# An even layer's gated unit, moved from ahead of its dilated attention to the attention's last heads

## The chip, the cores and the metric

The kernel runs on one core of one Trainium2 chip. The metric is the device time of one execution in microseconds; the kernel before has a median of 4341.29 us over three runs (4339.98 to 4341.60).

## The reference, cut to what matters

The program is two blocks one after the other. The change concerns the even layer of the second block, on 1024 tokens of width 1024:

```python
def mixer_even(h, pos, w_in, gmlp_norm, w_s, b_s, w_out):
    q, k, v, z = split(h @ w_in, [768, 1536, 2304])          # 12 heads of 64, z: 512 columns
    q, k = partial_rope(q), partial_rope(k)
    a_out = dilated_mixture(q, k, v)                          # 768 columns
    g_out = spatial_gating(z, gmlp_norm, w_s, b_s)            # 256 columns
    return concatenate([a_out, g_out]) @ w_out

def spatial_gating(z, v_norm, w_s, b_s):
    u, vv = split(gelu(z), 2)                                 # 256 columns each, 4 groups of 64
    vv = rmsnorm(vv, v_norm)                                  # over the 64 of each group
    mixed = einsum('gpq,bnqgc->bnpgc', w_s, vv) + b_s         # over the 128 tokens of a chunk
    return u * mixed
```

`dilated_mixture` joins three banded softmax attentions (dilations 1, 4 and 16) by their log-sum-exps.

## The kernel before, in words

The program states its operations in one order, and a tile scheduler that simulates time gives every engine its own queue from that; each engine then runs its queue in order. Tiles come from pools. A pool opened late stands where an earlier one was, so its first tile waits until the earlier one is closed.

All projections are products of fp32 numbers split in two: `split_into` (L98, L99) casts a tile to a high part on ACT and takes the rest on DVE or POOL, and `mm3` (L91 to L93) sums three partial matmuls. `proj_N` takes one projection of 128 tokens to 256 columns: 8 parts of the depth times 3, that is 24 matmuls; this is a *step* here. Weights come by `whalf` (L114) into `wraw` and are cast to `whi` and `wlo`.

Attention (`even_attn`) runs 12 heads of 8 *units*: four units of near keys (`near`, L1311) and four of keys of the same class mod 4 (`same_class`, L1319); four units are a half head here. A unit scores two tiles into a bank `ps` (four matmuls), takes the row maxima with the table of bands `tab` on DVE (L1361), the exps on ACT (L1364), turns the weights on PE (`pt`, L1328), splits them (L98, L99) and multiplies by the values (`po`, L1377 and L1389). Behind each unit, `step(unit)` runs what the table `order` holds for it. `plan(unit, n, *steps)` (L1282) fills the table: of the query and key pairs (`P[1]` to `P[5]`, two heads each) eight projection steps and four stacks at 16i-20 and 16i-8, of the value groups `V[1]` and `V[2]` (four heads each) eight steps at units 4 and 36, one step a unit. Pair 0 and V[0] stand in `order[-1]`, ahead of the first unit:

```python
        plan(4, 1, *V[1])
        plan(36, 1, *V[2])
        def step(unit):
            for f in order.get(unit, ()):
                f()
        step(-1)
        s2 = between()
        tab = s2.tile([128, 1152], F32, name="tab")
```

The gated unit (`even_gmlp`, L1123 to L1174) is stated before all of that. Its projections run up to the `yield` through `next(gmlp)` (16 steps, 384 matmuls, with gelu at the copy out of PSUM, L1129), partly in the tail of the MLP of the block ahead; the rest (norm of `vv`, mixing `pm`, the product with `u`, L1165, four transposes a time into `pzt` and the copy to `zo`, L1172) runs in `between()`, after pair 0 and V[0] and before the pool `eb` opens, from which `tab`, the values and the softmax tiles come. Its rows go to `eD`, the DRAM buffer from which the output projection reads. `by_class` sorts tokens by their class mod 4.

PSUM has one bank for the pairs' projections and stacks (`pj`), three banks under the tag "s" (`mb`: scores `ps`, projections of V, before also of z and the mixing), and the banks of `pt` and `po`. A pair of V steps (u = 0 and 1) shares one bank `mb`, taken by the first and freed by the copy behind the second. At the end, `last()` closes the pool of activations (`he`) and fetches and casts the rows of w_out.

Of the kernel before, what the change touches and what calls it, by code (L numbers as in the profile page):

```python
# [6 lines left out]
F32 = mybir.dt.float32  # L7
# [11 lines left out]
NT = 8  # L19
# [7 lines left out]
class Kern:  # L27
# [1095 lines left out]
    def even_gmlp(self, hT, w, dst, sp, W2):  # L1123

        nc, a = self.nc, self.a
        zz = []
        for i in range(2):
            z = sp.tile([128, NT, 256], F32, name="z%d" % i)
            self.proj_N2(self.w256(w, 2304 + 256 * i, W2 if i else None), hT, lambda t2, p: nc.scalar.activation(  # L1129
                z[:, 2 * t2:2 * t2 + 2, :], p, AF.Gelu_apprx_tanh), self.mb)  # L1130
            zz.append(z)
        yield
        self.exp_ln_table()
        u, vv = zz
        grow = self.row(a["even_gmlp_norm_2"], 256, "zg", sp)
        sq = sp.tile([128, NT, 256], F32, name="zsq")
        ss = sp.tile([128, 32], F32, name="zss")
        rs = sp.tile([128, 32], F32, name="zrs")
        nc.gpsimd.tensor_tensor(sq, vv, vv, op=ALU.mult)
        v32 = lambda x: x.rearrange("p t (g c) -> p (t g) c", g=4)  # L1140
        nc.vector.tensor_reduce(out=ss, in_=v32(sq), axis=AX.X, op=ALU.add)
        self.rstd(ss, 64, rs)
        nc.vector.tensor_tensor(v32(vv), v32(vv), rs[:, :, None].to_broadcast([128, 32, 64]), op=ALU.mult)
        nc.gpsimd.tensor_tensor(vv, vv, grow[:, None, :].to_broadcast([128, NT, 256]), op=ALU.mult)
        ws = sp.tile([128, 4, 128], F32, name="zws")
        for c in range(4):
            nc.sync.dma_start(ws[32 * c:32 * c + 32], dap(a["even_w_spatial_2"], 128 * c,
                                                          [[512, 32], [128 * 128, 4], [1, 128]]))
        br = sp.tile([4, 128], F32, name="zbr")
        nc.sync.dma_start(br, a["even_b_spatial_2"][0])  # L1150
        ws, br = self.by_class(ws, sp, "zwc"), self.by_class(br[:, None, :], sp, "zbq")[:, 0, :]
        p = self.tp("pws")
        for g in range(4):
            nc.tensor.transpose(p[:, g, :], ws[:, g, :], self.ident)
        wt = sp.tile([128, 4, 128], F32, name="zwt")
        nc.vector.tensor_copy(wt, p)
        p = self.tp("pbs")
        nc.tensor.transpose(p[:, 0, 0:4], br, self.ident[0:4, 0:4])
        bc = sp.tile([128, 4], F32, name="zbc")
        nc.vector.tensor_copy(bc, p[:, 0, 0:4])  # L1160
        for g in range(4):
            p = self.mb("pm").rearrange("p (t c) -> p t c", t=NT)
            gs = slice(g * 64, (g + 1) * 64)
            nc.tensor.matmul(p, wt[:, g, :], vv[:, :, gs], start=True, stop=True)
            nc.vector.scalar_tensor_tensor(sq[:, :, gs], p, bc[:, g:g + 1], u[:, :, gs], op0=ALU.add, op1=ALU.mult)  # L1165
        for i in range(2):
            o = sp.tile([128, 1024], F32, name="zo", tag="zo", bufs=1)
            for g in range(2):
                p = self.tp("pzt")
                for t in range(4):  # L1170
                    nc.tensor.transpose(p[:, t, :], sq[:, 4 * g + t, i * 128:(i + 1) * 128], self.ident)
# [10 lines left out]
    def even_attn(self, hT, w, dst, s1, W2, between, last):  # L1182
# [99 lines left out]
        def plan(unit, n, *steps):  # L1282
            for i, f in enumerate(steps):
                order.setdefault(max(unit + n * i, 0), []).append(f)
# [904 lines left out]
```

## Time and profile before

| | |
|---|---|
| median of 3 runs | 4341.29 us (4339.98 to 4341.60) |
| the profiled execution, its own time | 4346.24 us |
| its span in the profile | 4344.5 us |
| busy: PE, DVE, ACT, POOL | 3861.5 (89%), 2440.4 (56%), 1915.9 (44%), 1149.2 us (26%) |
| granted TensorE clock, 40 slices | 0.7 to 0.9 of full speed |
| the even layer's heads | first row maximum at 2209.70 us, last at 2596.71 us |

How to read it: the span begins at 0, and every time in microseconds is counted from there. A busy PE is no proof of full speed: matmuls are pipelined. The chain that ended last is 27% PE by itself, and the even layer is about an eighth of the span, so shares over the whole span say little of it; it is read by windows.

### The profile page before, as it was taken

Reading aid. Unit: us, or ns where it says so; the run is one execution under the profiler, and the core shown is the slowest. Engines: PE = TensorE matmul, PEld = TensorE weight load, DVE = VectorE, ACT = ScalarE, POOL = GpSimd, SP = SyncE. Lnnn points to the kernel's source line nnn. Section 1 sums busy time; section 2 is a strip of 40 time slices with the busy share of each in tenths; the row PEclk is TensorE's granted clock in tenths of the full one; section 3 lists DMA queues with packets and bytes.
Section 4 is the critical chain, followed back from the end, with each engine's and each line's share of the span. In section 5 each row is a group of like instructions: output and inputs, shape, how many; then the busy total and the mean of one; then the engine's idle time right before and its main releaser. Section 6 shows DMA issues by size and latency. Waiting matters only on the chain. (4 is left out here: it accounts for less than half of the span.)

```text
span 4344.5 us, 57369 instructions
## 1 busy us (share of the span) xinstructions
PE 3861.5 (89%) x21765; PEld 3209.0 (74%) x21765; DVE 2440.4 (56%) x4070; ACT 1915.9 (44%) x3190; POOL 1149.2 (26%) x878
## 2 busy tenths in 40 slices
PE   6999978898799999998999988699895898996997
PEld 5887866666587888886899977576694787884765
DVE  6545584663344233336446673787538566736876
ACT  3444434241424211112455662366523667832765
POOL 2000041330343112124412221011024556620111
PEclk8999989989899999999899998799997999997999
DMA  4212253121543111112242333799410001036997
GB/s 167 72 51 56 85 177 102 49 99 54 203 146 97 54 44 54 44 49 80 61 120 74 85 88 128 280 377 361 150 45 9 18 8 58 19 103 248 375 356 245
DMA packets 321975, 531.40 MB, mean 122 GB/s; under 512 B 39894, under 2 KB 217441, under 8 KB 321700
## 3 DMA queue, kind: packets, MB, share of 16 engines
q1 hardware_dynamic: 312052, 492.62, 33.5%
q0 software_dynamic: 9648, 35.13, 3.2%
q8 instruction: 171, 2.80, 0.3%
q14 instruction: 104, 0.85, 0.1%
HBM read 427.39 MB, written 91.88 MB: 120 GB/s over the span
## 5 line engine op out<-in xcount | busy, mean ns | idle before, releaser
L98 ACT ACTIVATE whi<-wraw 128x1024 fp32r<-128x1024 f32 (+1 forms) x515 | 530.1, 1038 | 777.7 <-PE py L93 213.7
L99 DVE TENSOR_TENSOR wlo<-wraw,whi 128x1024 fp32r<-128x1024 f32 (+3 forms) x418 | 519.0, 1258 | 409.6 <-ACT whi L98 397.2
L99 POOL TENSOR_TENSOR wlo<-wraw,whi 128x1024 fp32r<-128x1024 f32 (+3 forms) x97 | 226.6, 2336 | 1198.0 <-ACT whi L98 1135.7
L91 PE MATMUL pj<-h,whi 128*128 128x512 f32 (+1 forms) x592 | 255.6, 432 | 44.0 <-ACT gst L791 41.8
L92 PE MATMUL mm<-h,whi 128*128 128x512 f32 x640 | 253.9, 397 | 3.0 <-POOL h L99 1.8
L91 PE MATMUL mm<-h,whi 128*128 128x512 f32 x640 | 252.7, 397 | 1.8 <-ACT ms L905 1.4
L93 PE MATMUL mm<-h,wlo 128*128 128x512 f32 x640 | 252.9, 396 | 0.8 <-POOL wlo L99 0.8
L92 PE MATMUL pj<-h,whi 128*128 128x512 f32 (+1 forms) x592 | 248.1, 419 | 0.0
L93 PE MATMUL pj<-h,wlo 128*128 128x512 f32 (+1 forms) x592 | 246.5, 416 | 0.2 <-POOL wlo L99 0.2
L91 PE MATMUL pgu<-whi,xe 128*128 128x512 f32 x512 | 207.6, 406 | 6.2 <-ACT xe L98 6.2
L927 DVE TENSOR_TENSOR Y<-py,Y 128x1024 f32<-128x1024 f32 x112 | 137.1, 1224 | 133.3 <-PE py L93 133.3
L91 PE MATMUL py<-whi,mr 128*128 128x512 f32 x512 | 201.6, 394 | 9.3 <-DVE mr L936 8.2
L93 PE MATMUL pgu<-whi,xe 128*128 128x512 f32 x512 | 205.7, 402 | 0.0
L92 PE MATMUL pgu<-wlo,xe 128*128 128x512 f32 x512 | 205.5, 401 | 0.0
L93 PE MATMUL py<-whi,mr 128*128 128x512 f32 x512 | 203.1, 397 | 0.0
L92 PE MATMUL py<-wlo,mr 128*128 128x512 f32 x512 | 202.4, 395 | 0.0
L396 PE MATMUL ptp<-ident,e 128*128 128x128 f32 x1280 | 183.8, 278 | 15.1 <-ACT pf L400 6.9
L1038 DVE TENSOR_REDUCE ast<-ps 128x1 f32<-128x1024 f32 x128 | 156.4, 1222 | 69.7 <-PE ps L93 48.6
L91 PEld LDWEIGHTS pj<-h,whi 128*128 128x128 f32 (+1 forms) x592 | 118.4, 200 | 85.4 <-ACT gst L791 50.7
L396 PEld LDWEIGHTS ptp<-ident,e 128*128 128x128 f32 x1280 | 149.9, 143 | 30.8 <-ACT pf L400 13.6
L402 POOL TENSOR_TENSOR pt<-pf,pt 128x512 fp32r<-128x512 f32 x128 | 164.0, 1281 | 10.4
L99 DVE TENSOR_TENSOR pt<-ptp,pt 128x512 fp32r<-128x512 f32 x192 | 130.5, 689 | 40.2 <-ACT pt L98 38.9
(643 smaller groups left out, 11038.2 us busy)
## 6 DMA issues: line engine op xcount, KB each, us to landing
wraw<-in_moe_w_gate_dram SPq DMA_DIRECT2D x128, 512.0 KB
wraw<-in_moe_w_up_dram SPq DMA_DIRECT2D x128, 512.0 KB
wraw<-in_moe_w_down_dram SPq DMA_DIRECT2D x128, 512.0 KB
wraw<-in_mlp_w_dram SPq DMA_DIRECT2D x64, 512.0 KB
wraw<-in_w_in_dram SPq DMA_DIRECT2D x52, 512.0 KB
wad<-in_ada_w_dram SPq DMA_DIRECT2D x48, 512.0 KB
gD<-gst SPq DMA_DIRECT2D x24, 512.0 KB
wraw<-x SPq DMA_DIRECT2D x20, 512.0 KB
```

The source lines that it names most:

```text
L91: t.matmul(out, l[0], r[0], start=start, stop=False)
L92: t.matmul(out, l[0], r[1], start=False, stop=False)
L93: return t.matmul(out, l[1], r[0], start=False, stop=stop)
L98: nc.scalar.activation(hi, src, AF.Copy)
L99: (nc.gpsimd if leng == "pool" else nc.vector).tensor_tensor(lo, src, hi.bitcast(F32), op=ALU.subtract)
L396: nc.tensor.transpose(p[:, k, :], e[:, (4 * kg + k) * 128:(4 * kg + k + 1) * 128], self.ident)
L402: nc.gpsimd.tensor_tensor(lo, f, hi.bitcast(F32), op=ALU.subtract)
L927: nc.vector.tensor_tensor(y, pv, y, op=ALU.add)
L1038: nc.vector.tensor_reduce(out=st[:, 0:1], in_=pv, axis=AX.X, op=ALU.min)
```

## The change

The gated unit is no longer computed ahead of attention. `even_gmlp` and `by_class` go. Its two projections become `z_steps(1)` (the `vv` half) and `z_steps(0)` (the `u` half), eight steps each in the table, from unit 67 on, each pair of steps in a bank `mb`, copied without gelu to a tile `zs` and written to a DRAM buffer `zD`. `gated()` returns nine steps: `load` (unit 87) reads `zD` back, sorted by class through its addressing, together with the spatial weights, and applies gelu; `norm` (two halves, units 89, 90), `mix` (four groups, units 90 to 93) and `turn` (two, units 93, 94) compute the rest in the bank `pj`, in tiles that the query and key stacks no longer use. The spatial weights and biases are laid out by class and transposed beforehand, when inputs are prepared.

The table changes too: the pairs' eight projection steps are 1.5 units apart instead of 1, V[1] starts at unit 6 and V[2] at 34, both 3 units apart. The pool `eg` goes, and so does the gated unit's place in `between()`.

```diff
-    def even_gmlp(self, hT, w, dst, sp, W2):
...
-    def by_class(self, x, sp, name):
...
-        rests = [[s1.tile([128, 1024], FR, name="kl%d%d" % (i, j)) for j in range(2)] for i in range(2)]
+        rests = [[s1.tile([128, 1024], FR, name="kl%d%d" % (i, j), tag="kl%d%d" % (i, j)) for j in range(2)] for i in range(2)]
...
+        zD = self.dram.tile([1024, 512], F32, name="zD")
+        def z_steps(q):
+            wl, ps = [], []
+            def part(j):
+                i, u = divmod(j, 2)
+                if j == 0:
+                    wl.extend(self.w256(w, 2304 + 256 * q))
+                if u == 0:
+                    ps.append(self.mb())
+                self.proj_N(wl, hT, 2 * i + u, ps[0][:, u * 256:(u + 1) * 256])
+                if u == 0:
+                    return
+                z = s1.tile([128, 1024], FR, name="zs", tag="vs").bitcast(F32)[:, 0:512]
+                nc.scalar.activation(z, ps.pop(), AF.Copy)
+                nc.sync.dma_start(dap(zD, 256 * i * 512 + 256 * q, [[512, 128], [128 * 512, 2], [1, 256]]),
+                                  z.rearrange("p (u m) -> p u m", u=2))
+            return [lambda i=i: part(i) for i in range(8)]
+        def gated():
+            r = []
+            st = s1.tile([128, 2, 2, 16], F32, name="zst")
+            def load():
+                f, o = [s1.tile([128, 1024], F32, name="zf%d" % j, tag="kl0%d" % j) for j in range(2)]
+                wt, grow, bc = f[:, 0:512].rearrange("p (g t) -> p g t", g=4), f[:, 512:768], f[:, 768:772]
...
+                V = [s1.tile([128, 4, 2, 128], F32, name="zv", tag="eqk", bufs=2).rearrange("p t a b -> p t (a b)")
+                     for _ in range(2)]
+                U = [s1.tile([128, 1024], FR, name="zu", tag=n, bufs=3).bitcast(F32).rearrange("p (t m) -> p t m", t=4)
+                     for n in ("Q", "K")]
+                r.extend((U, V, o, wt, grow, bc))
+                for q, x in ((1, V), (0, U)):
+                    for g in range(2):
+                        nc.sync.dma_start(x[g], dap(zD, 512 * g * 512 + 256 * q, [[512, 128], [128 * 512, 4], [1, 256]]))
+                for x in V + U:
+                    nc.scalar.activation(x, x, AF.Gelu_apprx_tanh)
+                self.exp_ln_table()
+            def norm(g):
...
+                nc.gpsimd.tensor_tensor(sq, v, v, op=ALU.mult)
+                nc.vector.tensor_reduce(out=ss, in_=h4(sq), axis=AX.X, op=ALU.add)
+                self.rstd(ss, 64, rs)
+                nc.vector.tensor_tensor(h4(v), h4(v), rs[:, :, None].to_broadcast([128, 16, 64]), op=ALU.mult)
+                nc.gpsimd.tensor_tensor(v, v, grow[:, None, :].to_broadcast([128, 4, 256]), op=ALU.mult)
+            def mix(k):
+                U, V, o, wt, grow, bc = r
+                p = self.pj().rearrange("p (t c) -> p t c", t=NT)
+                gs = slice(k * 64, (k + 1) * 64)
+                for g in range(2):
+                    nc.tensor.matmul(p[:, 4 * g:4 * g + 4], wt[:, k, :], V[g][:, :, gs], start=True, stop=True)
+                for g in range(2):
+                    nc.vector.scalar_tensor_tensor(U[g][:, :, gs], p[:, 4 * g:4 * g + 4], bc[:, k:k + 1], U[g][:, :, gs],
+                                                   op0=ALU.add, op1=ALU.mult)
+            def turn(i):
+                o = r[2]
+                for g in range(2):
+                    p = self.pj().rearrange("p (t j) -> p t j", t=4)
+                    for t in range(4):
+                        nc.tensor.transpose(p[:, t, :], r[0][g][:, t, i * 128:(i + 1) * 128], self.ident)
+                    nc.scalar.activation(o[:, g * 512:(g + 1) * 512].rearrange("p (t j c) -> p t c j", t=4, c=4),
+                                         p.rearrange("p t (c j) -> p t c j", c=4), AF.Copy)
+                nc.sync.dma_start(dst[768 + i * 128:768 + (i + 1) * 128, :], o)
+            steps = lambda f, n: [lambda i=i: f(i) for i in range(n)]
+            return [load] + steps(norm, 2) + steps(mix, 4) + steps(turn, 2)
...
-                order.setdefault(max(unit + n * i, 0), []).append(f)
+                order.setdefault(max(unit + int(n * i), 0), []).append(f)
...
-            plan(16 * i - 20, 1, *p[0:8])
+            plan(16 * i - 20, 1.5, *p[0:8])
             plan(16 * i - 8, 1, p[8], p[10], p[9], p[11])
-        plan(4, 1, *V[1])
-        plan(36, 1, *V[2])
+        plan(6, 3, *V[1])
+        plan(34, 3, *V[2])
+        plan(67, 1.25, *z_steps(1), *z_steps(0))
+        z = gated()
+        plan(87, 1, *z[0:1])
+        plan(89, 1, *z[1:3])
+        plan(90, 1, *z[3:7])
+        plan(93, 1, *z[7:9])
...
-        sg = opn("eg")
-        gmlp = self.even_gmlp(h, a["even_w_in_2"], eD, sg, W2)
-        next(gmlp)
         T = []
         def between():
-            for _ in gmlp:
-                pass
-            cls("eg", "ew")
+            cls("ew")
             return opn("eb")
```

How the queues stand. First SP's, at the start of the layer, behind the last writes of the MLP (`x_82`). Before (`ecs` are the rotary tables, `zg`, `zws`, `zbr` the gated unit's inputs, `vD` the writes of values, `eD<-zo` the gated rows):

```order
L1004 DMA x_82<-Y 128x1024 x8
L114 DMA wraw<-in_even_w_in_dram 128x4x256 x2
L1192 DMA ecs_14238<-in_rope_even_dram 32x8x8 x4
L1192 DMA ecs_14243<-in_rope_even_dram 32x8x8 x4
L146 DMA zg<-in_even_gmlp_norm_dram 128x256
L1147 DMA zws<-in_even_w_spatial_dram 32x4x128 x2
L114 DMA wraw<-in_even_w_in_dram 128x4x256 x2
```

```order
L1272 DMA vD_14256<-vs 32x2x512 x5
L1174 DMA eD<-zo 128x1024
L371 DMA K_14516<-K_14516 64x4x128
L371 DMA K_14517<-K_14517 64x4x128
L1174 DMA eD<-zo 128x1024
L1298 DMA tab<-in_even_bands_dram 128x1152
```

And now:

```order
L1004 DMA x_82<-Y 128x1024 x8
L1133 DMA ecs_13809<-in_rope_even_dram 32x8x8 x4
L1133 DMA ecs_13814<-in_rope_even_dram 32x8x8 x4
L114 DMA wraw<-in_even_w_in_dram 128x4x256 x2
L1213 DMA vD_13827<-vs 32x2x512 x4
L114 DMA wraw<-in_even_w_in_dram 128x4x256 x2
L1213 DMA vD_13827<-vs 32x2x512
L371 DMA K_14089<-K_14089 64x4x128
L1213 DMA vD_13827<-vs 32x2x512
L371 DMA K_14090<-K_14090 64x4x128
L1213 DMA vD_13827<-vs 32x2x512 x6
L1323 DMA tab<-in_even_bands_dram 128x1152
```

The fetch of `tab` moved ahead of the last writes of values, and the first weights of V (`wraw`, 128x4x256) behind the eight loads of `ecs`.

Second ACT's queue. Before, in the layer's start, the gelus (`z<-mb`) stand in one stretch, with table loads around it and around the norm:

```order
L98 ACTIVATE he_13338<-ms 128x256 x15
L1129 ACT_TABLE_LOAD
L1129 ACTIVATE z_13812<-mb 128x512 x3
L98 ACTIVATE whi<-wraw 128x1024 x3
L1129 ACTIVATE z_13812<-mb 128x512
L98 ACTIVATE whi<-wraw 128x1024
L1129 ACTIVATE z_14025<-mb 128x512 x3
```

Now, in head 10 (`e` are exps of the softmax, `P` their split parts, `zs` a copied pair of z steps):

```order
L98 ACTIVATE P_18611<-pt 128x512
L1389 ACTIVATE e,sA<-e,sA 128x256
L98 ACTIVATE P_18695<-pt 128x512
L1258 ACT_TABLE_LOAD
L1258 ACTIVATE zv<-zv 128x1024
L1233 ACTIVATE zs<-mb 128x512
L1389 ACT_TABLE_LOAD
L1389 ACTIVATE e,sA<-e,sA 128x256 x2
L1364 ACTIVATE oAB<-po 64x512
```

A gelu (`zv`) stands between exps, with a table load ahead of it and one behind; heads 9 to 11 hold 12 such loads.

Third PE's queue in head 10, between the same-class and the near units. Before:

```order
L1319 MATMUL ps<-K_18376,Qc 128x256
L1319 MATMUL ps<-kl_14248,Qc 128x256
L1311 MATMUL ps<-K_18377,Q_18341 128x256
L1311 MATMUL ps<-kl_14249,Q_18341 128x256
L1389 MATMUL po<-P_19001,vc 128x256
L1328 MATMUL pt<-ident,e 128x128 x3
```

Now, of near units (L1336 scores, L1353 transposes):

```order
L1336 MATMUL ps<-K_18837,Q_18776 128x256
L1336 MATMUL ps<-kl_13821,Q_18776 128x256
L1353 MATMUL pt<-ident,e 128x128 x2
L92 MATMUL mb<-wlo,he_13338 128x256
L93 MATMUL mb<-whi,he_13339 128x256
L91 MATMUL mb<-whi,he_13338 128x256
L92 MATMUL mb<-wlo,he_13338 128x256
L93 MATMUL mb<-whi,he_13339 128x256
L1353 MATMUL pt<-ident,e 128x128 x2
L1336 MATMUL ps<-K_18837,Q_18776 128x256
L1336 MATMUL ps<-kl_13821,Q_18776 128x256
```

Matmuls of a z step (`mb`) now stand between a unit's transposes and the next scores.

## Rows read from the trace of the kernel before

**Rows 1.** Windows: stretch, its us, busy per engine (instructions), PE clock, DMA share, GB/s.

```profile
2100.00:2120.00 20.00, 15.22 (x108) 14.82 (x107) 5.75 (x11) 10.84 (x19) 14.21 (x16) 0.83 0.32 80
2120.00:2140.00 20.00, 20.00 (x172) 20.00 (x171) 1.93 (x3) 2.69 (x4) 1.49 (x1) 1.00 0.39 102
...
2300.00:2320.00 20.00, 17.97 (x142) 16.42 (x141) 15.77 (x53) 16.28 (x42) 8.42 (x9) 1.00 0.31 90
2320.00:2340.00 20.00, 16.52 (x104) 15.14 (x103) 16.64 (x52) 14.40 (x42) 2.58 (x2) 0.83 0.26 60
...
2520.00:2540.00 20.00, 12.88 (x61) 10.04 (x60) 17.53 (x31) 14.36 (x37) 9.70 (x8) 0.74 0.38 126
2540.00:2560.00 20.00, 15.76 (x86) 13.95 (x85) 16.61 (x46) 16.07 (x38) 7.56 (x4) 0.75 0.57 172
2560.00:2580.00 20.00, 17.59 (x132) 15.66 (x133) 18.79 (x60) 15.27 (x46) 4.11 (x3) 1.00 0.28 71
2580.00:2600.00 20.00, 16.97 (x125) 14.68 (x124) 17.36 (x57) 15.52 (x45) 4.65 (x3) 1.00 0.21 54
```

(The engines stand in the order PE, PEld, DVE, ACT, POOL.)

**Rows 2.** Windows: all twelve heads, and fifteen units at their end without projections.

```profile
2210.00:2597.00 387.00, 359.25 (x2824) 343.86 (x2823) 259.93 (x734) 241.65 (x625) 97.07 (x102) 0.96 0.33 89
2560.00:2597.00 37.00, 31.60 (x235) 27.80 (x236) 34.64 (x109) 28.16 (x82) 7.18 (x5) 1.00 0.23 60
```

**Rows 3.** DVE's timeline (start, us, engine, line): attention's first and last row maximum.

```profile
2209.70 0.42 DVE L1361 CUSTOM_DVE_ANT_0 e<-ps,tab 128x256 f32<-128x256 f32 x1 [9.55 <-ACT eqk L1236]
...
2596.71 0.41 DVE L1361 CUSTOM_DVE_ANT_0 e<-ps,tab 128x256 f32<-128x256 f32 x1
```

**Rows 4.** SP's timeline at the layer's start (issue of DMAs).

```profile
2109.79 0.94 SPq L114 DMA_DIRECT2D wraw<-in_even_w_in_dram  x2
2110.95 5.04 SPq L1192 DMA_DIRECT2D ecs<-in_rope_even_dram  x8
...
2205.68 0.34 SPq L1298 DMA_DIRECT2D tab<-in_even_bands_dram  x1
```

**Rows 5.** ACT's and POOL's timeline at the layer's start.

```profile
2108.98 1.28 ACT L1129 ACT_TABLE_LOAD   x1
2110.28 1.57 ACT L1129 ACTIVATE z<-mb 128x512 f32<-128x512 f32 x3
2113.63 1.06 ACT L98 ACTIVATE whi<-wraw 128x1024 fp32r<-128x1024 f32 x1 [1.78 <-DMA wraw<-in_even_w_in_dram]
2114.82 2.40 POOL L99 TENSOR_TENSOR wlo<-wraw,whi 128x1024 fp32r<-128x1024 f32 x1 [1.08 <-ACT whi L98]
```

**Rows 6.** PE's timeline: a wait in the MLP's tail, and attention's first value matmul.

```profile
2063.30 0.79 PE L91 MATMUL py<-whi,mr 128*128 128x512 f32 x1 [3.63 <-DVE mr L936]
...
2219.36 0.22 PE L1377 MATMUL po<-P,va 128*128 128x128 f32 x1
```

**Rows 7.** Groups by line, 2560.3 to 2597.1: count, busy, mean ns, idle before.

```profile
L1361 DVE CUSTOM_DVE_ANT_0 e<-ps,tab 128x256 f32<-128x256 f32 x30 | 12.3, 413 | 0.5 <-PE pt L1328 0.3
L1319 PE MATMUL ps<-K,Qc 128*128 128x256 f32 x16 | 5.8, 360 | 0.9 <-DVE sB L1361 0.9
```

**Rows 8.** The gated unit's tiles: least, median, longest ns; first and last start.

```profile
L1129 ACT ACTIVATE z<-mb x8: 592/599/603, 2110.3 to 2142.1; 128x512 f32<-128x512 f32 x8
L1165 DVE SCALAR_TENSOR_TENSOR zsq<-pm,zbc,z x4: 741/746/751, 2192.1 to 2196.3; 128x512 f32<-128x512 f32 x4
L1143 DVE TENSOR_TENSOR z<-z,zrs x1: 2291/2291/2291, 2153.8 to 2153.8; 128x2048 f32<-128x2048 f32 x1
```

**Rows 9.** Groups by line over the layer (ACT 2105 to 2640, DVE 2050 to 2720).

```profile
L98 ACT ACTIVATE whi<-wraw 128x1024 fp32r<-128x1024 f32 x28 | 29.5, 1057 | 22.1 <-PE pj L93 10.6 <-PE mb L93 4.9 <-DMA wraw<-in_even_w_out_dram 3.6
L1172 ACT ACTIVATE zo<-pzt 128x512 f32<-128x512 f32 x4 | 4.0, 1115 | 2.3 <-DMA eD<-zo 1.4 <-PE pzt L1171 0.9
L1129 ACT ACT_TABLE_LOAD x1 | 1.3, 1283 | 0.0
...
L1361 DVE CUSTOM_DVE_ANT_0 e<-ps,tab 128x256 f32<-128x256 f32 x192 | 76.6, 417 | 50.0 <-PE ps L1319 20.4 <-PE ps L1311 11.4 <-ACT eqk L1236 9.5
```

More of the change, by code (lines that the diff above doesn't have):

```diff
@@ L1121, in band_table @@
             nc.vector.tensor_tensor(o, o, ab, op=ALU.add)
-    def even_gmlp(self, hT, w, dst, sp, W2):
[L1125 to L1171, printed above, removed]
-                nc.scalar.activation(o[:, g * 512:(g + 1) * 512].rearrange("p (t j c) -> p t c j", t=4, c=4),
-                                     p.rearrange("p t (c j) -> p t c j", c=4), AF.Copy)
-            nc.sync.dma_start(dst[768 + i * 128:768 + (i + 1) * 128, :], o)
@@ L1176, in by_class @@
-    def by_class(self, x, sp, name):
-        y = sp.tile(list(x.shape), F32, name=name)
-        self.nc.vector.tensor_copy(y.rearrange("p a (c j) -> p a c j", c=4), x.rearrange("p a (j c) -> p a c j", c=4))
-        return y
     def even_attn(self, hT, w, dst, s1, W2, between, last):
@@ new lines, in gated @@
+        def gated():
[4 more added lines that the diff above has]
+                wt, grow, bc = f[:, 0:512].rearrange("p (g t) -> p g t", g=4), f[:, 512:768], f[:, 768:772]
+                nc.sync.dma_start(wt, a["even_w_spatial_2"])
+                nc.sync.dma_start(bc, a["even_b_spatial_2"])
+                nc.sync.dma_start(grow, dap(a["even_gmlp_norm_2"], 0, [[0, 128], [1, 256]]))
+                V = [s1.tile([128, 4, 2, 128], F32, name="zv", tag="eqk", bufs=2).rearrange("p t a b -> p t (a b)")
[10 more added lines that the diff above has]
+            def norm(g):
+                v = r[1][g]
+                o, grow = r[2], r[4]
+                sq = o.rearrange("p (t m) -> p t m", t=4)
+                h4 = lambda x: x.rearrange("p t (h c) -> p (t h) c", h=4)
+                ss, rs = st[:, g, 0], st[:, g, 1]
+                nc.gpsimd.tensor_tensor(sq, v, v, op=ALU.mult)
[23 more added lines that the diff above has]
+            return [load] + steps(norm, 2) + steps(mix, 4) + steps(turn, 2)
@@ L2178 @@
                                     np.zeros((128, NT))], 1).astype(bf16)
+    q = 4 * (p % 32) + p // 32
+    w = np.asarray(inputs["even_w_spatial_2"]).reshape(4, 128, 128)
+    data["even_w_spatial_2"] = np.ascontiguousarray(w[:, q][:, :, q].transpose(2, 0, 1))
+    data["even_b_spatial_2"] = np.ascontiguousarray(np.asarray(inputs["even_b_spatial_2"]).reshape(4, 128)[:, q].T)
     arrays, a = {}, {}
```

## The prediction
> **What bounds the kernel now.** I read in this order: twenty-microsecond slices of the even layer, one window over its twelve heads, the timelines at the stage's two ends, and the rows of single operations.
>
> The slices [rows 1] show two kinds of time. Where projections run between the pieces of attention (2120 to 2140, and most slices up to 2520), PE is busy 20.00 of 20 us and starts 172 matmuls: one costs 20/172, about 0.115 us. Where the plan has no projections, PE starts 61 to 142 a slice, the granted clock falls as low as 0.74, and DVE is busy 15.8 to 18.8 us: there attention is bound by DVE and by the chain of score, softmax, transpose and values. The gated unit's two projections, 384 matmuls, stand ahead of everything, in the full kind of slice; the empty ones come at units 20 to 27, 52 to 59 and from 68 to the end. Over all heads, 2210 to 2597, PE starts 2824 matmuls [rows 2], worth 325 us at 0.115, in 387 us. Some 60 us lie idle, and the change offers them 384 matmuls, 44 us of work.
>
> The first row maximum of attention is taken at 2209.70, the last at 2596.71 [rows 3]. The first waits behind the gated unit in two ways: PE runs its matmuls, and the table of bands (`tab`) is fetched only at 2205.68 [rows 4], since its pool opens after the gated unit's has closed.
>
> **The sum, part by part.** Durations are those of the profiled execution (4346.24 us, span 4344.50). The median of the runs, 4341.29, is 5 us lower; I take differences off the median. Less than 0.2% (8.7 us) cannot be told from no change here.
>
> *Start.* Before, 144 of the 384 gated matmuls run inside the MLP's tail, in three PSUM banks, and 240 after it. Now pair 0 projects first, into the one bank `pj`, and only 48 matmuls fit there; from the last input at 2109.8 to the first score the order has 348 matmuls, 40.0 us. They are not all ready. The first values projection needs weights whose fetch now stands behind eight small loads (`ecs`) on SP, 5.04 us; from such an issue at 2109.79 to the first cast at 2113.63 it took 3.84 us [rows 4, 5]. Then a cast of 1.06 on ACT and 2.40 on POOL [rows 5]: ready at 2109.8 + 5.0 + 3.8 + 1.1 + 2.4 = 2122.1. Till then PE has just 48 matmuls. The other 300 take 34.5 us: 2156.6, and about 3 more because the clock is 0.83 around 2100 to 2120 [rows 1]. First maximum at 2160, against 2209.7: **-50 us**. Ends: 2150 if the weights never wait (2109.8 + 40), 2175 if the 9.55 us that DVE idled before its first maximum [rows 3] and some more come back. The 14 pair-0 matmuls that now stand ahead of the MLP's last `py` groups cost nothing: PE waits 3.63 us there for DVE [rows 6].
>
> *First values.* The reads of values (`va`) follow the last writes of values. Before, the first value matmul came at 2219.36 [rows 6], 9.7 us after the first maximum. Now PE has one pair of projection steps (48 matmuls, 5.5 us) to fill that with: a hole of 4.2, **+4 us**; ends 0 and +10.
>
> *The heads.* A half head (four units) without projections is measured at the end: 30 row maxima, so 15 units, in 2560.3 to 2597.1 [rows 7], 9.8 us a half head; in it run 235/15 x 4 = 63 matmuls [rows 2], 7.2 us. A projection step is 24 matmuls, 2.76 us. So a half head with n steps takes the larger of 9.8 and 7.2 + 2.76n. Steps per half head, counted in the order between the score matmuls, before: 6, 6, 3.5, 2.5, 4, 2, 0, 0, 4, 8, 3.6, 2.4, 4, 2, 0, 0, 4, 4, and six of 0: 56 steps, 353 us by the formula, 387 measured. The 34 missing (weight casts, stacks, in-order waits) I keep. After: 4, 4, 2, 2, 1.3, 0.7, 4, 6, 8, 2, 2, 1.1, 0.9, 4, 4, 2, 2, 10, 3.7, 3.1, 3.2, 2, 0, 0: 72 steps, 377 us. So +24 us for 16 steps that cost 44 by themselves. The scheduler bunches what the plan spreads (ten steps in one half head), so it isn't less.
>
> *The gated unit.* Its norm falls in half heads of 2 or 3 steps, which PE bounds, and hides there: a reduction and a product, 2.29 us over 2048 columns [rows 8], each now in two halves. The eight products after the mixing fall in the last two half heads, which DVE bounds: 0.746 us for 512 columns [rows 8], now 256; I take 0.4, so 3.2 (ends 3.0 and 6.0). **Heads and unit: +27 us.** From below: all 3232 matmuls at 0.115 are 372 us, -15. From above: nothing hides, 44 and 6, +50.
>
> *DMA and tail.* Eight writes of `zD` and four reads add some nine issues of 0.5 us to SP, which idles far longer. Cover of the round trip: units 85 to 95, 11 x 2.45 = 27 us, against a copy, two DMA landings of some 3 us, and a gelu; without it the output projection would wait for the unit's rows. The w_out casts (8 on ACT, 1.06 each [rows 9]) must wait until the activations' pool is free, now at unit 85 instead of 68; they stay hidden if ACT has room (below). Tail: 0; ends -5 and +8.
>
> Sum: -50 + 4 + 27 = **-19 us: 4322**.
>
> **Rivals.**
>
> *More gain, 4305.* The idle time is filled better than the formula says. For it: of the 34 us of loss a good part stood where the clock was 0.74 [rows 1], and there z steps run now. Against: the bunching. Heads and unit at +10 instead of +27 give -36. Below 4300 if the heads near PE's floor.
>
> *Little gain, 4335: ACT bounds the last heads.* Gelu moves between the softmaxes' exps: the order has 12 table loads in heads 9 to 11 where the unit had 4, at 1.283 us each [rows 9]. Plain attention keeps ACT busy 28.16 us in 15 units [rows 2], 7.5 a half head, 45 in the last six. Add the loads (15.4), four gelus at a cast's 1.06 (4.2), eight z copies at 0.6 (4.8), eight casts (8.5) and four turned copies (4.5) [rows 8, 9]: 82 us, where formula and share of the loss give those six 90. It just fits; if half of the loads, gelus and copies (13 us) stop the chain, the gain is 6. The Trainium skill, page "ScalarE: Activation LUTs", section "Rules for kernel authors", speaks against this part of the change: group functions by table set, and budget about 2.7 us for every switch. Here the rows show a load of 1.28 with the gelu 0.02 us behind it [rows 5]; by the page's figure ACT would need 82 + 12 x 1.4 = 99 us, 9 over the 90, and the result would be 4331.
>
> *No change, 4345: steps add instead of overlapping.* PE runs in order; a step between a score and its transposes lets DVE wait. Then a half head takes 9.8 + 2.76n: 390 us before, which is near the 387 measured, and 434 after. For it: that agreement. Against: in full slices PE starts 172 matmuls with DVE's work in the same 20 us, so they do overlap. +44 and 3 for the heads leave -50 + 4 + 47 = +1, and the late start end makes the rest.
>
> *Slower, 4368: the score banks.* Scores use three PSUM banks; a V or z pair of steps borrows one from its first matmul to its copy. Before, the pair's two steps were planned in neighbouring units, now 3 apart for V, and in the order they stand 1 to 3.5 units apart, together some 30 units on two banks. Then a unit can wait for its own scores, 0.36 [rows 7] and three times 0.115, and its two maxima of 0.41 stand alone: 1.5 x 30 = +46. It decides from 28/30 = 0.9 us a unit. For it: DVE waits 31.8 us for scores already [rows 9]. Against: two banks still let one unit be scored while another is read.
>
> *That it doesn't do what it says*: partly so, as the step counts show; it is in the sum.
>
> **How the numbers follow.** Forecast (4310 to 4332) 0.47, more gain 0.23, little (4331 to 4341) 0.10, none (to 4350) 0.10, slower 0.10. The range 4300 to 4341 leaves out about 0.07 below and, with the last two cases part of which fall inside, 0.13 above; it takes in the ends of the start (-10, +15). Faster by over 0.2% (below 4332.6): 0.47 + 0.23 + half of little, 0.75. Slower (over 4350): 0.10. Within: 0.15.
>
> **What would show it.** First row maximum near 2160, last near 2578; 72 steps in between, slices of 160 or more matmuls in most of heads 8 to 10, a low clock only in head 11. ACT busy under 85% in the last three heads. The unit's rows written before head 11's. Wrong if DVE waits for scores (`ps`) by more than today's third of a microsecond a unit, if the first maximum comes after 2175, or if PE waits for the gated unit's rows in the output projection.

## The result, and the profile after

The change makes the kernel slower: a median of 4375.15 us against 4340.66 us, 1.0077 times (95% interval 1.0055 to 1.0098). Its profiled execution has a span of 4380.1 us, against 4344.5. The forecast said 4322.

The start came as forecast, the heads did not. DVE's timeline of the changed kernel, first and last row maximum (line 1386 now), against [rows 3]:

```profile
2164.07 0.42 DVE L1386 CUSTOM_DVE_ANT_0 e<-ps,tab 128x256 f32<-128x256 f32 x1 [1.04 <-DMA tab<-in_even_bands_dram]
...
2629.25 0.41 DVE L1386 CUSTOM_DVE_ANT_0 e<-ps,tab 128x256 f32<-128x256 f32 x1
```

Attention starts 45.6 us earlier and lasts 465.2 us in place of 387.0, that is 78.2 us longer. From the last maximum to the first matmul behind the routing that follows the layer it is 40.9 us (43.4 before), so that matmul starts at 2670.1 in place of 2640.1.

Windows of the changed kernel (columns as in [rows 1]): the MLP's tail, all heads, two pieces of them, and a slice of head 11. Below them the tail before the change.

```profile
2040.00:2120.00 80.00, 46.92 (x223) 36.98 (x223) 53.84 (x84) 38.17 (x87) 43.75 (x44) 0.74 0.19 67
2164.00:2630.00 466.00, 430.59 (x3304) 413.54 (x3305) 279.88 (x764) 276.40 (x668) 110.80 (x108) 0.94 0.33 92
2316.00:2346.00 30.00, 29.06 (x221) 28.39 (x221) 4.66 (x21) 7.06 (x16) 3.59 (x7) 0.91 0.02 5
2469.00:2499.00 30.00, 29.03 (x245) 28.59 (x244) 8.34 (x29) 9.03 (x22) 4.50 (x8) 1.00 0.18 46
2600.00:2620.00 20.00, 15.39 (x84) 12.66 (x83) 15.79 (x39) 19.07 (x43) 7.84 (x5) 0.84 0.40 126
```

```profile
2040.00:2120.00 80.00, 59.53 (x326) 51.38 (x325) 53.94 (x85) 43.57 (x93) 48.87 (x45) 0.83 0.21 73
```

Three things are to be seen. The tail of the MLP runs 103 matmuls fewer. The heads have 3304 matmuls where they had 2824 [rows 2]; the 480 more are worth 55 us at 0.115, but the heads grew by 78, so the idle time that was to be filled grew too. And in two pieces of 30 us, at the start of heads 4 and 8, PE does little but projections while DVE is busy 4.66 and 8.34 us: attention stands.

The group of row maxima over the layer, against [rows 9]:

```profile
L1386 DVE CUSTOM_DVE_ANT_0 e<-ps,tab 128x256 f32<-128x256 f32 x192 | 77.6, 418 | 74.5 <-PE ps L1336 36.1 <-PE ps L1344 19.4 <-PE pt L1353 16.6
```

DVE waits 55.5 us for scores (`ps`), 31.8 before. Why PE has pieces of eight steps in a row shows in the timelines. SP fetched pair 2's raw weights from 2202; ACT cast the second half of them right behind V[1]'s last matmul on PE, and the first half 1.5 us earlier (SP's, ACT's and PE's timelines):

```profile
2202.01 8.28 SPq L114 DMA_DIRECT2D wraw<-in_even_w_in_dram  x16
```

```profile
2257.69 1.04 ACT L98 ACTIVATE whi<-wraw 128x1024 fp32r<-128x1024 f32 x1
```

```profile
2257.34 0.28 PE L93 MATMUL mb<-whi,he 128*128 128x256 f32 x1
```

All projections in the heads take their weights from the pool `wp` with two buffers of `whi` and two of `wlo`, and each job (a pair, a values group, half of z) needs both. V[1], spread over units 6 to 27, holds them until unit 27; pair 2, planned for units 12 to 22, waits, runs its 192 matmuls from 2259.6 to 2289.1 with little between them, and its stacks come when head 4 already needs them. The piece in head 4 is pair 3's: its weights are cast only when pair 2 is at its end, and its matmuls, behind pair 2's stacks in the one bank `pj`, run from 2316.8 to 2344.9 with only a few of attention's between them. The piece in head 8 is pair 5's, which stands behind V[2] and pair 4 in the same way. ACT's and DVE's timelines, pair 3's first cast and the row maximum of head 4 that waits for that piece to end:

```profile
2288.01 1.06 ACT L98 ACTIVATE whi<-wraw 128x1024 fp32r<-128x1024 f32 x1 [2.95 <-PE pj L93]
```

```profile
2345.61 0.42 DVE L1386 CUSTOM_DVE_ANT_0 e<-ps,tab 128x256 f32<-128x256 f32 x1 [11.60 <-PE ps L1336]
```

That is theory A: the spacing costs, through the weight buffers. Its rival, theory B: the gated unit itself costs, by its ACT work and the extra steps in heads 9 to 11.

### The profile page after: what moved, and what is told of

The parts are those of the page before. It is cut to its first block, busy times and chain, and to the rows that moved or that the text cites. A ratio compares the mean times of both kernels' runs of the same rounds, so it can differ in the third digit from the quotient of the medians.

```text
span 4380.1 us, 57411 instructions
## 1 busy us (share of the span) xinstructions
PE 3871.9 (88%) x21768; PEld 3220.0 (74%) x21768; DVE 2447.4 (56%) x4076; ACT 1928.9 (44%) x3204; POOL 1150.2 (26%) x880
```

## The experiments

The runs, by their ratio to the kernel before on the same chip (95% interval), and by three times of their profiled executions: first and last row maximum, and PE's first matmul behind the routing. What follows that matmul varies between executions by up to 11 us whatever was edited, so the three times, each of one execution, say where, and the ratio says how much. Lengths of heads and half heads below are counted from the second row maximum of one to the second of the next (to the last maximum, in head 11).

| run | ratio | first | last | PE resumes |
|---|---|---|---|---|
| kernel before | 1 | 2209.7 | 2596.7 | 2640.1 |
| the change | 1.0077 (1.0055 to 1.0098) | 2164.1 | 2629.2 | 2670.1 |
| old_spacing | 0.9994 (0.9983 to 1.0006) | 2163.9 | 2593.7 | 2637.2 |
| spread_only | 1.0029 (1.0019 to 1.0039) | 2211.9 | 2612.4 | 2655.1 |
| disjoint | 1.0010 (0.9999 to 1.0020) | 2165.6 | 2604.9 | 2648.2 |
| v_old | 1.0031 (1.0018 to 1.0044) | 2162.5 | 2608.5 | 2651.7 |
| p_old | 1.0036 (1.0024 to 1.0048) | 2165.2 | 2613.2 | 2656.8 |
| v_held | 1.0049 (1.0031 to 1.0067) | 2162.5 | 2624.7 | 2668.9 |
| no_gelu | 1.0035 (1.0022 to 1.0048) | 2162.6 | 2613.9 | 2655.4 |
| old_no_gelu | 0.9989 (0.9977 to 1.0001) | 2165.3 | 2592.3 | 2635.2 |
| thin_z | 0.9999 (0.9987 to 1.0012) | 2158.2 | 2589.6 | 2632.9 |
| no_rest | 0.9996 (0.9982 to 1.0010) | 2165.9 | 2588.3 | 2629.4 |
| no_rest_thin | 0.9949 (0.9932 to 0.9967) | 2159.9 | 2562.9 | 2606.2 |
| grouped | 0.9985 (0.9973 to 0.9997) | 2166.0 | 2604.0 | 2633.2 |
| z_mid_grouped | 1.0005 (0.9993 to 1.0017) | 2160.0 | 2592.7 | 2634.6 |
| z1_first_grouped | 1.0045 (1.0028 to 1.0061) | 2190.8 | 2611.0 | 2654.0 |
| z1_first_early | 1.0031 (1.0018 to 1.0045) | 2189.2 | 2612.6 | 2655.6 |
| v0_first | 1.0035 (1.0021 to 1.0049) | 2173.6 | 2608.3 | 2639.2 |

### The two parts of the change, one at a time

old_spacing keeps the moved unit and puts the table's spacing back:

```diff
-            plan(16 * i - 20, 1.5, *p[0:8])
+            plan(16 * i - 20, 1, *p[0:8])
-        plan(6, 3, *V[1])
-        plan(34, 3, *V[2])
+        plan(4, 1, *V[1])
+        plan(36, 1, *V[2])
```

> The changed kernel with the old table for pairs and values (all steps one unit apart, V[1] at 4, V[2] at 36); the gated unit stays in the last heads. Theory A (two weight buffers): each job of projections (a pair, a values group, half of z) needs both buffers of whi and wlo, so a job whose steps are 3 units apart holds them for 24 units, the pair planned beside it waits and then runs in one piece, 7 or 8 steps in a row, while attention stands; without that, heads 3, 4, 7 and 8 lose their pieces and the kernel is about 30 us faster than the changed one, 4335 to 4350. Theory B (the gated unit itself is what costs: ACT and the extra steps in heads 9 to 11): about 4370, within 8 us of the changed kernel.

It stands at 0.9994, so the spacing costs the changed kernel 0.83%, 36 us of 4345, and the moved unit alone is worth nothing that can be measured. Theory A gave this; theory B did not. The heads of the two profiles differ by 35 us: 22 lie in heads 0 to 8 (355.6 against 333.7 us from the first maximum), where the late pieces are, and 13 in heads 9 to 11 (109.6 against 96.1).

spread_only is the kernel before with the new spacing, the reverse of the diff above.

> The kernel before with only the new spacing of pairs and values; the gated unit stays ahead of attention. Theory A: the same late pieces as in the changed kernel, so 20 to 30 us slower than before, 4360 to 4370. Theory B: 4335 to 4345, no difference from before, or some us less if the spread fills idle slots as it is meant to.

1.0029, 12.6 us: slower as A said, less than it said. The same late pieces are there (head 3 takes 52.9 us, where it took 27.6 before), but the heads between them are shorter. So of the 36 us that the spacing costs the changed kernel, some 23 come only with the moved unit.

### Which spacing, and is it the spacing or what it holds

v_old puts back only the values' spacing, p_old only the pairs'.

> The changed kernel with the values groups back at units 4 and 36, one unit apart, and the pairs still 1.5 apart. Theory A (a values group whose steps are 3 units apart holds both weight buffers for 24 units, and the pair planned beside it comes late and in one piece): nearly all of the 30 us that the old spacing won, so within 10 us of the kernel before. Theory D (the pairs' spacing is what brings their stacks of queries and keys late, ending at 16i-9.5 where the stacks are planned at 16i-8): most of the loss stays, 20 to 35 us slower than before.

> The changed kernel with the pairs one unit apart as of old, and the values groups still 3 apart at units 6 and 34. Theory A: the loss stays, 22 to 35 us slower than before; DVE's idle time ahead of scores stays above 50 us and heads 3, 4 and 8 stay the longest. Theory D: within 10 us of before.

Neither theory has it alone: 1.0031 and 1.0036. Each spacing costs about 0.4% by itself, the two together 0.83%. In p_old heads 3, 4 and 8 are the long ones (52.9, 53.5 and 59.7 us), as in the changed kernel. In v_old the heads 9 to 11 are 10 us longer than in old_spacing (105.7 to 96.1) and the rest of the loss lies in heads 4 and 8.

disjoint has pairs 3 to 5 still 1.5 apart, but no two jobs at the same units:

```diff
-            plan(16 * i - 20, 1.5, *p[0:8])
+            plan(16 * i - 20, 1 if i < 3 else 1.5, *p[0:8])
-        plan(6, 3, *V[1])
-        plan(34, 3, *V[2])
-        plan(67, 1.25, *z_steps(1), *z_steps(0))
+        plan(4, 1, *V[1])
+        plan(20, 1, *V[2])
+        plan(71, 1, *z_steps(1), *z_steps(0))
```

> The changed kernel with a table in which no two jobs overlap: V[1] at 4 and V[2] at 20, one unit apart, pairs 1 and 2 one unit apart, pairs 3 to 5 still 1.5 apart, z from 71 one unit apart. Theory A: the pieces are gone as in old_spacing, and the spread pairs fill some idle time: 4330 to 4345. If it is the distance between a pair's two steps by itself that costs (a bank or a matmul row split by attention, theory C), the 1.5 spacing left in pairs 3 to 5 keeps about half of the loss: 4355 to 4365. Theory B: about 4370.

1.0010: between the ranges of A and of C (that the distance between a pair's two steps costs by itself), nearer to A's. Pairs 1.5 apart cost little where nothing else is planned beside them. It moves z and V[2] too, so it does not prove the pairs' share.

v_held is old_spacing with four steps of 72 moved:

```diff
-        plan(4, 1, *V[1])
-        plan(36, 1, *V[2])
+        plan(4, 1, *V[1][:6])
+        plan(26, 1, *V[1][6:])
+        plan(36, 1, *V[2][:6])
+        plan(54, 1, *V[2][6:])
```

> The changed kernel with the old spacing, but for the last pair of steps of each values group, which is put off to units 26 and 54; the other six steps run at 4 to 9 and 36 to 41. Only four of 72 steps are moved. Theory A (the group keeps both weight buffers until its last step, so pairs 2 and 4 can't have their weights cast before units 27 and 55 and then run in one piece, against the start of heads 4 and 8): 10 to 20 us slower than with the old spacing, as with all of the values' steps 3 units apart. If it is the 3 units between steps that cost (attention's matmuls in between, a bank held): within 4 us of the old spacing.

1.0049, 24 us slower than old_spacing, more than A's 10 to 20, and no less than with all values steps 3 apart (p_old; the intervals overlap). This is the run that decides for the values: six of eight steps run early, no two steps of a pair stand apart, and the loss is there, with the group still holding its weights. Values that come late are not the reason: in v_held no idle time of PE ahead of a value matmul ends with a read of values, only with the split weights of the softmax. SP's and ACT's timelines of v_held, and ACT's of old_spacing, for pair 2's weights:

```profile
2197.76 7.92 SPq L114 DMA_DIRECT2D wraw<-in_even_w_in_dram  x16
```

```profile
2265.63 1.04 ACT L98 ACTIVATE whi<-wraw 128x1024 fp32r<-128x1024 f32 x1
```

```profile
2231.60 1.05 ACT L98 ACTIVATE whi<-wraw 128x1024 fp32r<-128x1024 f32 x1
```

The first cast starts 60 us after the last of the fetches was issued; with the old spacing it comes 34 us earlier. What the runs don't part is the second link of the chain, from pair 2 to pair 3: its weights, and the bank `pj` that pairs share with their stacks. No run has a second bank `pj`.

### What the moved unit pays for the start's 45 us

With the old spacing the heads still last 429.8 us, 42.8 more than before. Three runs, all with the old spacing, take the moved work apart. thin_z cuts the z steps, no_rest leaves out what follows them, no_rest_thin does both (shortened):

```diff
-                self.proj_N(wl, hT, 2 * i + u, ps[0][:, u * 256:(u + 1) * 256])
+                self.proj_N(wl[:1], hT, 2 * i + u, ps[0][:, u * 256:(u + 1) * 256])
```

```diff
-            def load():
...
-            return [load] + steps(norm, 2) + steps(mix, 4) + steps(turn, 2)
+            def turn(i):
+                o = s1.tile([128, 1024], F32, name="zf1", tag="kl01")
+                nc.sync.dma_start(o, dap(zD, i * 128 * 1024, [[1024, 128], [1, 1024]]))
+                nc.sync.dma_start(dst[768 + i * 128:768 + (i + 1) * 128, :], o)
+            return steps(turn, 2)
```

> The changed kernel with the old spacing, and each of the 16 z steps cut from 24 matmuls to 3 (one of the eight parts of the depth, so the gated rows are made from an incomplete projection); copies, DMAs, gelus and the rest of the unit stay. 336 matmuls are gone, 14 steps' worth. If a step in the heads costs its whole 2.76 us: 35 to 40 us faster than with the old spacing. If attention hides them, as the forecast's larger-of-two formula has it (9.8 against 7.2 + 2.76 n a half head): about 25 us or less. If ACT and DVE bound the last heads: under 15 us.

> The changed kernel with the old spacing and without the rest of the gated unit: no gelu, norm, mixing, product or turning; its rows are read from zD and written on as they are. The z steps and their copies stay. Theory E (the rest is what the last heads pay for, by ACT, DVE and the waits it puts into their queues): 20 to 30 us faster than with the old spacing, resume of PE behind the layer near 2612. Theory F (the moved steps are what is paid for, 2.76 us each): within 8 us of the old spacing.

> The same, with the z steps cut to 3 matmuls each as well. Theory E: the z steps lie beside attention or are paid back by the clock they keep up, as the run with thin z and the whole rest showed: within 8 us of the run without the rest. Theory F: 30 us or more below it. If the steps are hidden only while the rest holds ACT and DVE up (both bound the same time, the longer decides): 10 to 25 us below it.

Against old_spacing's 0.9994: without 336 matmuls 0.9999, without the rest 0.9996, without both 0.9949. Taken alone neither is worth anything; taken together they are worth 20 us. The forecasts that gave either a price of its own fail over the three runs together (no_rest alone fits theory F's 8 us, thin_z alone the 15 us that were set for ACT and DVE as the bound); the last clause of the third expectation holds. The windows over heads 9 to 11, of the kernel before, old_spacing, thin_z, no_rest and no_rest_thin in this order:

```profile
2525.00:2597.00 72.00, 57.92 (x372) 50.47 (x371) 64.22 (x180) 53.83 (x142) 19.43 (x13) 0.87 0.36 107
```

```profile
2498.00:2594.00 96.00, 85.67 (x644) 81.12 (x643) 70.83 (x189) 77.17 (x164) 31.30 (x16) 0.95 0.38 117
```

```profile
2483.00:2590.00 107.00, 79.10 (x441) 69.30 (x439) 80.98 (x201) 83.45 (x179) 29.26 (x17) 0.78 0.42 131
```

```profile
2503.00:2589.00 86.00, 77.91 (x619) 74.95 (x618) 61.98 (x172) 57.58 (x148) 23.41 (x13) 0.96 0.43 126
```

```profile
2485.00:2563.00 78.00, 60.60 (x399) 52.79 (x398) 66.81 (x181) 61.36 (x160) 22.97 (x14) 0.89 0.54 168
```

With both, PE is busy 85.67 of 96 us and ACT 77.17. Without the z matmuls PE has 441 where it had 644, the granted clock falls from 0.95 to 0.78, and the three heads last 107 us: what head 8 wins (37.7 in place of 48.9 us) they give back. Without the rest PE still has 619 matmuls, busy 77.91 of 86. Only without both do the heads come near the 72 us of before.

no_gelu (the changed kernel) and old_no_gelu (with the old spacing) put copies in place of the gelus:

```diff
-                    nc.scalar.activation(x, x, AF.Gelu_apprx_tanh)
-                self.exp_ln_table()
+                    nc.scalar.activation(x, x, AF.Copy)
```

> The changed kernel with plain copies in place of the four gelus and without the table of exp and ln asked for behind them, so the gated unit's result is without gelu; all else as it is. Theory A: the table loads lie mostly beside other work: 0 to 5 us faster than the changed kernel, 4370 to 4375. Theory B: up to eight loads of 1.283 us leave the chain of the last heads: 8 to 15 us faster, 4360 to 4367.

> The changed kernel with the old spacing, with copies in place of the four gelus and without the table asked for behind them; the rest of the unit stays. If the gelus' table loads are the larger part of the rest's price: 10 to 15 us faster than with the old spacing, as in the changed kernel; if they cost only where the late pieces had crowded the last heads: under 5 us.

In the changed kernel 0.42% (18 us) is won, a little over what theory B gave; with the old spacing 0.05%, which is nothing. The gain lies in heads 9 to 11: 96.3 us in no_gelu for 109.6, which is what old_spacing takes (96.1) with the same twelve table loads. Late pieces ahead of these heads don't make them long (p_old 96.4, v_held 97.5); they are long where the last pairs are 1.5 apart (v_old 105.7, disjoint 113.4). So 13 of the 35 us go with the pairs' spacing and the gelus together, and not with what the values hold; which wait carries them is not shown. ACT's groups by line in the changed kernel, 2480 to 2640:

```profile
L1258 ACT ACT_TABLE_LOAD x4 | 5.1, 1283 | 1.8 <-DMA zv<-zD 1.7
L1389 ACT ACT_TABLE_LOAD x4 | 5.1, 1283 | 0.1
```

Four more (L166, L167, L59) are as long each. Twelve loads, 15.4 us, as the order had said.

### Attempts at a version that is faster

grouped is old_spacing with the gelus tied:

```diff
+                zc = s1.tile([128, 1], F32, name="zc")
+                nc.vector.tensor_scalar(zc, V[0][:, 0, 0:1], 0.0, 0.0, op0=ALU.mult, op1=ALU.add)
+                for x in [V[1]] + U:
+                    nc.vector.scalar_tensor_tensor(zc, x[:, 0, 0:1], 0.0, zc, op0=ALU.mult, op1=ALU.add)
-                    nc.scalar.activation(x, x, AF.Gelu_apprx_tanh)
+                    nc.scalar.activation(x, x, AF.Gelu_apprx_tanh, bias=zc)
```

> The changed kernel with the old spacing, and the four gelus tied together: each takes as its bias a column of zeros that is made from all four tiles, so that none starts before the last has landed, and the table is loaded once for the four and once back. If ten table loads of 1.283 us stand on the chain of the last heads, 8 to 13 us faster than with the old spacing alone, and so as much faster than the kernel before; if they mostly lie beside other work, or if what went with the gelus in the run without them was their order and not the loads, 0 to 4 us.

0.9985 (0.9973 to 0.9997): the only whole version below the kernel before, by 6 us, which is less than the 0.2% named in the prediction. Against old_spacing it is 4 us, not told apart from it, though its last heads hold 2 table loads where old_spacing's hold 12.

Three more start from grouped. z_mid_grouped plans `z_steps(1)` at unit 20 and `z_steps(0)` at 52, one unit apart. The other two project `z_steps(1)` ahead of pair 0, with weights from the pool of V[0] (`W2`), `z_steps(0)` from unit 68, and z1_first_early also moves the rest three to six units ahead:

```diff
-                    wl.extend(self.w256(w, 2304 + 256 * q))
+                    wl.extend(self.w256(w, 2304 + 256 * q, W2 if q else None))
...
-        order[-1] = p[0:6] + p[8:9] + p[6:8] + p[10:11] + v[0:2] + p[9:10] + v[2:4] + p[11:12] + v[4:8]
+        z1 = z_steps(1)
+        order[-1] = z1 + p[0:6] + p[8:9] + p[6:8] + p[10:11] + v[0:2] + p[9:10] + v[2:4] + p[11:12] + v[4:8]
...
-        plan(67, 1.25, *z_steps(1), *z_steps(0))
+        plan(68, 1.25, *z_steps(0))
```

> As the one with tied gelus, with the z steps in the two stretches where the old table has no projections, units 20 to 27 and 52 to 59, one unit apart; the rest of the gated unit stays in the last heads, and the w_out casts go back to heads 8 and 9. If a step costs its 2.76 us wherever it is put (the sum 9.8 + 2.76 n for a half head), the same time as with tied gelus in the last heads, within 5 us. If the middle's empty stretches hide steps better than the last heads, where ACT is busy too, 8 to 15 us faster than that, 15 to 25 us faster than before.

> Tied gelus and the old spacing, with the first half of z (z_steps(1), 192 matmuls) projected first of all, where the tail of the MLP leaves PE idle and three banks are free (144 gated matmuls ran there before the change), with the weights from the pool of V[0]; only z_steps(0) stays in the heads, from unit 68. If the tail hides 144 of the 192 and a step in the heads costs 2.76 us: the first row maximum some 5 us later, the heads 20 us shorter, so 12 to 17 us faster than with tied gelus alone and 15 to 25 us faster than the kernel before. If pair 0 loses the same slots in the tail that z gains: no gain over tied gelus, within 5 us.

> The same with the rest of the gated unit six units earlier, loading from unit 81 and turning at 90 and 91. If the end of head 11 is crowded by the unit's DVE and ACT work, 3 to 8 us faster than the run with the rest at unit 87; if that work costs the same wherever it stands, the same within 4 us.

The middle is no better a place: 1.0005, 9 us slower than grouped, where the same time or a gain was forecast. z first is a miss, 1.0045 and 1.0031 (not told apart): the tail of the MLP took none of it (222 matmuls from 2040 to 2120 in z1_first_grouped, 223 in the changed kernel), so the first maximum came at 2190. Its weights came from the later pool, which opens when the MLP's have closed.

v0_first is grouped with V[0] ahead of pair 0 and their weight pools exchanged:

```diff
-                    wl.extend(self.w256(w, 1536 + 256 * q, None if q else W2))
+                    wl.extend(self.w256(w, 1536 + 256 * q))
...
-                                          for k in range(4) for c in (0, 768)])
+                                          for k in range(4) for c in (0, 768)], W=None if pair else W2)
...
-        order[-1] = p[0:6] + p[8:9] + p[6:8] + p[10:11] + v[0:2] + p[9:10] + v[2:4] + p[11:12] + v[4:8]
+        order[-1] = v[0:8] + p[0:6] + p[8:9] + p[6:8] + p[10:11] + p[9:10] + p[11:12]
```

> Tied gelus and the old spacing, with V[0] projected first of all, from the weight pool that is free during the MLP's tail, and pair 0 after it with the weights of the later pool. Three banks take V[0]'s steps where pair 0 has the one bank, so the tail should again hide some 144 matmuls (as it did with the gated unit's before the change) in place of 48: the first row maximum 10 to 14 us earlier than the changed kernel's 2164, and the first values ready before it. 12 to 18 us faster than tied gelus alone, 18 to 25 us faster than the kernel before. If the two heads behind the start take the time back (the same steps, only earlier, and the same last heads): within 5 us of tied gelus alone.

A window of v0_first, the MLP's tail:

```profile
2040.00:2120.00 80.00, 58.38 (x314) 50.28 (x313) 52.51 (x85) 39.33 (x86) 45.36 (x44) 0.81 0.20 67
```

The tail does hide 91 matmuls more than in the changed kernel, so what it had lost went with the one bank and the pool (both are changed here, so which of them isn't shown). But pair 0's weights now come late (its first matmul is at 2124.85, after 5.96 us of waiting for their cast), the first maximum at 2173.6, and the ratio is 1.0035: 22 us slower than grouped, where 12 to 18 us faster was forecast.

## Why the prediction was wrong

- **The start**, forecast at 2160: measured 2164.1, within its ends. The working held too: weights ready at 2122.1 by the sum, and the split on POOL ended at 2121.98. In the tail 144 gated matmuls less 48 of pair 0 would be 96 fewer; it has 103 fewer.
- **The first values**, +4: the first value matmul came at 2176.26, 12.2 us after the first maximum, and the first half head took 27.7 us, 3.9 more than its six steps give (7.2 + 16.6). Right in size, but not by the way that was thought: PE waited only 1.11 us for the values, and the 48 matmuls ahead of them took 8.3 us in place of 5.5, since the granted clock was 0.51 from 2164 to 2171. That part is luck.
- **The heads**, +27: measured +78. This step failed: "a half head with n steps takes the larger of 9.8 and 7.2 + 2.76n", with the loss of 34 us kept as it was. The counts of steps from the order were right. With steps counted between row maxima, the formula gives 337 us for the first 23 half heads before, 370 in the changed kernel and 377 with the old spacing; they took 381, 449 and 421. So the loss over the formula is 44 us before, 44 with the old spacing, and 80 in the changed kernel: 36 us of the 78 are the loss that was thought to stay, 32 the formula's (24 in the forecast), 10 the last half head. Three half heads hold 35 of the 80: the end of head 3 (2.0 steps) took 23.8 us where the formula gives 12.7, the start of head 4 (8.6 steps) 42.5 where it gives 31, that of head 8 (8.0 steps) 41.2 where it gives 29. The order was read as a count for each half head, and not for what stands in it one behind the other: eight steps in a row, with the scores done and the transposes behind them, are no cover for attention. The bunching was seen and written down; why it was there (two weight buffers that jobs planned side by side can't share) was not looked for, so its lateness had no price. By old_spacing the price of the new spacing is 36 us, by the profiles 22 of 35 in heads 0 to 8, where the pieces are. That the formula fits old_spacing doesn't prove it: in thin_z it gives 347 us, and 424 were measured.
- **The gated unit**, hidden but for 3.2 us: the heads with the old spacing are 42.8 us longer for 467 matmuls more up to the resume, and the start won 45.8 (2163.9 for 2209.7). So the move by itself came out even (0.9994): shown. Of the z matmuls and the rest, taking either away wins nothing that can be measured, taking both 20 us.
- **The tail**, 0: measured -2.5 in the changed kernel. Right.
- **Rival "steps add"** (434 us of heads): old_spacing's 430 agrees with the sum, but its mechanism does not stand: 14 steps' worth of matmuls taken away changed nothing. The agreement was one of numbers.
- **Rival "score banks"** (4368, slower): nearest in time, and its sign was there, DVE's waits for scores up by 23.7 us. But v_held, where the values' steps stand one unit apart, loses no less than p_old, so a bank held across units isn't needed to explain it. For the z steps the banks were not tried.
- **Rival "ACT bounds the last heads"**: half right. ACT is busy 19.07 of 20 us in a slice of head 11, and the gelus cost 18 us there, but only in the changed spacing. The Trainium skill, page "ScalarE: Activation LUTs", section "Rules for kernel authors", budgets about 2.7 us for a switch; the rows show 1283 ns for each load. Its advice to group by table set was followed only with the old spacing, in grouped, where it wins 4 us that can't be told from nothing; in the changed kernel no run shows what grouping is worth.

What stays open: why thin_z gives nothing. The clock fell with the matmuls, and the work of ACT and DVE is the same in both; how much of the 107 us is the clock and how much the rest's waits was not taken apart. Nor was the new spacing tried with a third pair of weight buffers, which would show theory A directly.

## What to carry to other kernels

When a plan spreads steps that use staged weights, the life of the buffers spreads with them: look up how many jobs can hold weights at once before two of them are planned side by side. Read a new order for runs of one kind of work in a row, and price a run as a stall of everything behind it. And before work is moved into idle time, ask whether that idle time is already the shadow of another cost: of two fillers that each fit, both together may not.

## What the hardware showed that was not expected

Less work came with a slower clock and won no time: from 2500 to 2580 the mean granted clock was 0.94 in old_spacing with 553 matmuls and 0.72 in thin_z with 306.

Small operations on DVE can last as long as POOL's. DVE's and POOL's timelines in z1_first_grouped, in the norm of the gated unit:

```profile
2557.04 3.61 DVE L165 TENSOR_SCALAR rsv<-zst 128x16 f32<-128x16 f32 x1
```

```profile
2556.42 1.90 POOL L1271 TENSOR_TENSOR zf<-zv 128x1024 f32<-128x1024 f32 x1
2558.27 2.35 POOL L99 TENSOR_TENSOR wlo<-wraw,whi 128x1024 fp32r<-128x1024 f32 x1
```

An operation on 16 columns, 0.16 us in the norm's other half, begins inside POOL's first and ends at 2560.65, 0.03 us behind POOL's second. The row maxima wait behind it. The Trainium skill, page "SBUF — State Buffer", section "Terms", says that VectorE and GpSimd share one pair of ports, held by one of them for a whole instruction; the trace agrees in that the wait ends with POOL's work, though here it lasts past one POOL operation to the end of the next. Over the heads of the changed kernel DVE's operations of at most 64 columns took 7 us more than the least duration of each (3 before), so this is a small part of the 78.
